# The level products of a gated recurrence, made for 64 of 128 columns

## The chip, the cores and the metric

The kernel runs on one core of a Trainium2 chip. The metric is the device time of one execution in microseconds (us); the runs of the kernel before took 2719.22 to 2722.33 us, with a median of 2722.05 us. In the profile PE is TensorE's matmul, PEld its loading of weights, DVE is VectorE, ACT is ScalarE, POOL is GpSimd and SP is the engine whose queue issues most DMAs.

## The reference

The model has two layers on 1024 tokens of 1024 features, all in fp32. Layer 0 mixes a short convolution with a gated linear recurrence of four heads (128 keys by 128 values each); layer 1 is a retention layer; each is followed by a feed-forward network. Only the recurrence is touched here. For each head and each chunk the reference computes

```python
b = jnp.cumsum(ln, axis=-2)                       # logs of the forget gates, summed along the chunk
diff = b[:, :, :, None, :] - b[:, :, None, :, :]
decay = jnp.exp(jnp.where(causal[:, :, None], diff, -jnp.inf))
scores = jnp.einsum('bhik,bhijk,bhjk->bhij', qn, decay, kn)
o_intra = jnp.einsum('bhij,bhjv->bhiv', scores, vn)
```

so that the score of query i and key j is a sum over 128 keys with a decay of its own for each pair (i, j).

## The kernel before

The tokens are worked on in two halves of 512 (`HT`), and each half in four chunks of 128 (`P`). `mixer0` first projects F (gates), K, Q and V of the half with `four` (lines 331 to 333), then runs the recurrence over the chunks (lines 349 to 423), and after that the convolution's projections (`feat`, lines 426 to 445) and the output products.

The score matrix S of a chunk, with keys j on partitions and queries i along the row, is put together from a diagonal (lines 356 to 359) and from seven levels, `LEVELS` = 1, 2, 4, ..., 64. At the level with spacing s the chunk's 128 tokens are cut into blocks of 2s; in each block the first s tokens act as keys and the last s as queries. The helper `two` gives these two interleaved views of a tile: 64 columns each, in runs of s with a gap of s between them (at s = 64 one run of 64). VectorE and ScalarE write both into one tile, `xs`: x1, the decayed queries, at the columns of the last s (line 369), and x0, the decayed keys, at the columns of the first s (lines 371 and 373).

TensorE then multiplies `xs` by itself, for each head a 128 x 128 product into a quarter of one PSUM bank (lines 375 and 376). `copy_predicated` (line 379) reads from this bank only the 64 columns of the last s, `two(sp)[1]`, and copies into S those that a mask allows. Lines 380 to 384 bring the running products of the gates, SF and F, to the next level, so the chain from level to level runs through VectorE; the products of a level only feed line 379.

In all there are 2 halves x 4 chunks x 7 levels = 56 such groups of 4 matmuls. In the trace each fp32 matmul stands as two records, each with a weight load of its own, so a group is 8 records and the line has 448.

The other products of the kernel (`mm3`, lines 149 to 151) take fp32 values as a sum of two fp32r parts and stand as one record of 512 columns each. Line 199 (in `scales`) multiplies 128 x 128 fp32 weights by a single column of ones, line 181 (in `spread`) multiplies fp32 weights by 512 columns, and line 398 transposes on TensorE.

The order of the instructions on each engine is not written out by hand. A planner takes the program's order as a priority, estimates each instruction's duration, and places on each engine's queue what it expects to be ready. So the convolution's products of lines 149 to 151 stand on TensorE's queue between the groups of line 376, although the code has them after the recurrence. On the chip each queue is then run in that fixed order.

Of the kernel before, what the change touches and what calls it, by code (L numbers as in the profile page):

```python
# [75 lines left out]
def trunk(ctx: ExitStack, tc: tile.TileContext, a: dict, out: bass.AP, decay):  # L76
# [19 lines left out]
    mm, vec, act = nc.tensor.matmul, nc.vector, nc.scalar  # L96
# [56 lines left out]
    def bank(name):  # L153
        return banks[name].tile([P, HT], F32, name=name)

    def rsqrt(x, n):

        it = sm.tile([P, n], I32, name="it")
        vec.tensor_scalar(it, x.bitcast(I32), 1, None, ALU.logical_shift_right)
        yi = sm.tile([P, n], I32, name="yi")  # L160
        vec.tensor_scalar(yi, it, -1.0, float(0x5F3759DF), ALU.mult, ALU.add)
        y = yi.bitcast(F32)
        for _ in range(3):
            t = sm.tile([P, n], F32, name="nt")
            vec.tensor_tensor(t, y, y, ALU.mult)
            u = sm.tile([P, n], F32, name="nu")
            vec.scalar_tensor_tensor(u, t, -0.5, x, ALU.mult, ALU.mult)
            z = sm.tile([P, n], F32, name="nz")
            vec.scalar_tensor_tensor(z, u, 1.5, y, ALU.add, ALU.mult)
            y = z  # L170
        return y
# [124 lines left out]
    def mixer0(ph, odd):  # L296
# [12 lines left out]
        for half in range(NH):  # L309
# [39 lines left out]
            for c in range(NC):  # L349
                first = half == 0 and c == 0  # L350
                cs = slice(c * P, (c + 1) * P)
                Fc, Kc, Qc = F[:, :, cs], K[:, :, cs], Q[:, :, cs]
                SF = ph.tile([P, HEADS, P], F32, name="SF")
                nc.gpsimd.memset(SF, 1.0)
                S = ph.tile([P, HEADS, P], F32, name="S")
                sp = bank("pa").rearrange("p (h i) -> p h i", i=P)
                for m in range(HEADS):
                    mm(sp[:, m], Kc[:, m], Qc[:, m], start=True, stop=True)
                vec.tensor_tensor(S, sp, ident.unsqueeze(1).to_broadcast([P, HEADS, P]), ALU.mult)
                for n, s in enumerate(LEVELS):  # L360
                    nb = P // (2 * s)

                    def two(t):
                        v = t.rearrange("p h (n w s) -> p h n w s", w=2, s=s)
                        return v[:, :, :, 0, :], v[:, :, :, 1, :]

                    xs = ph.tile([P, HEADS, P], F32, name="xs", bufs=3)
                    (x0, x1), (f0, f1), (k0, _), (_, q1), (s0, s1) = map(two, (xs, Fc, Kc, Qc, SF))
                    vec.tensor_tensor(x1, q1, f1, ALU.mult)
                    if s == 1:  # L370
                        act.copy(x0, k0)
                    else:
                        vec.tensor_tensor(x0, k0, s0, ALU.mult)
                    sp = bank("pa").rearrange("p (h i) -> p h i", i=P)
                    for m in range(HEADS):
                        mm(sp[:, m], xs[:, m], xs[:, m], start=True, stop=True)  # L376
                    mk = msk[:, n].rearrange("p (n w s) -> p n w s", w=2, s=s)[:, :, 1, :]
                    last = [P, HEADS, nb, s]
                    vec.copy_predicated(two(S)[1], mk.unsqueeze(1).to_broadcast(last), two(sp)[1])
                    if s == 1:  # L380
                        act.copy(s0, f1)
                    else:
                        vec.tensor_tensor(s0, s0, f1[:, :, :, s - 1 : s].to_broadcast(last), ALU.mult)
                    vec.tensor_tensor(f1, f1, f0[:, :, :, s - 1 : s].to_broadcast(last), ALU.mult)
                qd = ph.tile([P, HEADS, P], F32, name="xs", bufs=3)
                vec.tensor_tensor(qd, Qc, Fc, ALU.mult)
                op = bank("pb")
                for m in range(HEADS):
                    vs = slice(m * P, (m + 1) * P)
                    mm(op[:, vs], S[:, m], V[:, c, vs], start=True, stop=first)  # L390
                    if not first:
                        mm(op[:, vs], qd[:, m], state[:, m], start=False, stop=True)
                if half < NH - 1 or c < NC - 1:
                    kd = ph.tile([P, HEADS, P], F32, name="xs", bufs=3)
                    vec.tensor_tensor(kd, Kc, SF, ALU.mult)
                    tp = bank("pa")
                    for m in range(HEADS):
                        nc.tensor.transpose(tp[:, m * P : (m + 1) * P], kd[:, m], ident)
                    kt = ph.tile([P, HT], F32, name="xs", bufs=3)
                    act.copy(kt, tp)  # L400
                    up = bank("pb")
                    for m in range(HEADS):
                        vs = slice(m * P, (m + 1) * P)
                        mm(up[:, vs], kt[:, vs], V[:, c, vs], start=True, stop=True)
                    if first:
                        vec.tensor_copy(state, up.rearrange("p (h v) -> p h v", v=P))
                    else:
                        for m in range(HEADS):
                            vec.scalar_tensor_tensor(
                                state[:, m], state[:, m], Fc[:, m, P - 1 : P], up[:, m * P : (m + 1) * P], ALU.mult, ALU.add  # L410
                            )
                sq = ph.tile([P, HT], F32, name="t1", bufs=2)
                act.activation(sq, op, AF.Square)
                ss = sm.tile([P, HEADS], F32, name="ss")
                vec.tensor_reduce(ss, sq.rearrange("p (h v) -> p h v", v=P), AX.X, ALU.add)
                ms = sm.tile([P, HEADS], F32, name="ms")
                vec.tensor_scalar(ms, ss, 1.0 / P, EPS, ALU.mult, ALU.add)
                r = rsqrt(ms, HEADS)
                ot = ph.tile([P, HEADS, P], F32, name="on", bufs=4)
                vec.tensor_tensor(  # L420
                    ot, op.rearrange("p (h v) -> p h v", v=P), r.unsqueeze(2).to_broadcast([P, HEADS, P]), ALU.mult
                )
                on.append(ot)
# [694 lines left out]
    def mixer(layer):  # L1118
        with ExitStack() as es:
            if layer == 0:  # L1120
                new_h(0)
                new_h(2)
            es.enter_context(psum(mm=4, pa=2, pb=2))
            new_w(es, 1024, 3)
            new_x(es.enter_context(tc.tile_pool(name=f"mx{layer}", bufs=1, reuse_waits="tile")))
            if layer == 0:
                with tc.tile_pool(name="p0", bufs=1) as ph:
                    start(ph)
            else:
                apply(scaled_h[0], 0, R_MIX + NK)  # L1130
            with tc.tile_pool(name=f"mp{layer}", bufs=1, reuse_waits="tile") as ph:
                with tc.tile_pool(name=f"mo{layer}", bufs=1, reuse_waits="tile") as odd:
                    return (mixer1 if layer else mixer0)(ph, odd)
# [37 lines left out]
```

## Time and profile before

| | before |
|---|---|
| median of 3 runs | 2722.05 us |
| lowest and highest | 2719.22 and 2722.33 us |
| the profiled execution | 2720.06 us |
| its span from first to last instruction | 2718.3 us |
| PE busy | 2640.4 us (97%) |
| DVE busy | 1823.4 us (67%) |
| line 376, PE busy | 60.5 us |

The recurrence of the first half lies at 88 to 168 us of the span and that of the second half at 332 to 409 us. A matmul's busy time in a row overlaps with that of its neighbours, since matmuls are pipelined; the distance between starts, or between ends in the chain, is what one takes from TensorE's time.

### The profile page before, as it was taken

To read this page: it belongs to the slowest core of one execution; us is meant where nothing else is said; L and a number is where in the kernel's file an instruction comes from. 1 tells how busy PE (TensorE), PEld (TensorE's weight loads), DVE (VectorE), ACT (ScalarE), POOL (GpSimd) and SP (SyncE) were. 2 spreads that over 40 slices of the span, in tenths; PEclk is the share of its full clock that TensorE was granted. 3 is DMA by queue.
4 is the path that set the end of the run, shared out by engine and by line. 5 is a ranking of instruction groups with operands and counts; after the bars stand their busy time and mean duration, and the time that the engine had idled before them with its cause. 6 is when DMAs were issued, how large, how long until landed. Compare 5 with 4: busy or idle time off the path is not lost.

```text
span 2718.3 us, 32932 instructions
## 1 busy us (share of the span) xinstructions
PE 2640.4 (97%) x12093; PEld 2180.1 (80%) x12093; DVE 1823.4 (67%) x3387; ACT 1014.0 (37%) x1669; POOL 378.0 (14%) x282
## 2 busy tenths in 40 slices
PE   8999999979999999999999999999998899999998
PEld 6888888757877788878888888888886688888886
DVE  5786497666587666677667667567678666655665
ACT  5223313434434433343332333333344444443332
POOL 0000000042332313200000000000002323231320
PEclk9999999989999999999999999999999999999999
DMA  4224312344434477332322333322224444447742
GB/s 155 78 65 128 95 47 78 116 146 153 160 135 148 163 289 269 130 109 79 92 85 86 94 101 104 104 80 78 85 88 126 167 156 155 146 141 288 269 173 83
DMA packets 320498, 356.28 MB, mean 131 GB/s; under 512 B 11464, under 2 KB 246544, under 8 KB 319312
## 3 DMA queue, kind: packets, MB, share of 16 engines
q1 hardware_dynamic: 317808, 347.13, 38.6%
q0 software_dynamic: 1520, 5.51, 0.6%
q8 instruction: 95, 1.56, 0.2%
q10 hardware_dynamic: 1008, 1.54, 0.2%
q14 instruction: 67, 0.55, 0.1%
HBM read 268.15 MB, written 85.98 MB: 130 GB/s over the span
## 4 chain that ended last, share of the span: by engine, by line
PE 86%; DVE 5%; issue 3%; POOL 2%; DMA 2%; ACT 1%; POOLq 0%; ACTq 0%; DVEq 0%
PE mm L151 15%; PE mm L149 15%; PE mm L150 15%; PE sd L517 6%; PE sd L519 6%; PE sd L518 6%; PE mm L517 5%; PE mm L518 5%; PE mm L519 5%; PE pa L376 2%; POOL s L502 1%; DMA raw<-in_ffn_w_in 1%; DVE wlo L133 1%; DVE st L133 1%; POOL raw L505 1%
## 5 line engine op out<-in xcount | busy, mean ns | idle before, releaser
L136 ACT CAST whi<-raw 128x512 fp32r<-128x512 f32 (+2 forms) x604 | 454.1, 755 | 1115.0 <-PE mm L150 387.6
L133 DVE TENSOR_TENSOR wlo<-raw,whi 128x512 fp32r<-128x512 f32 (+2 forms) x604 | 541.8, 899 | 220.6 <-ACT whi L136 218.6
L149 PE MATMUL mm<-xe,whi 128*128 128x512 f32 x960 | 376.4, 393 | 1.5 <-ACT xe L136 1.5
L150 PE MATMUL mm<-xe,whi 128*128 128x512 f32 x960 | 376.9, 393 | 0.0
L151 PE MATMUL mm<-xe,wlo 128*128 128x512 f32 x960 | 376.3, 392 | 0.0
L517 PE MATMUL sd<-x,whi 128*128 128x512 f32 x640 | 254.0, 397 | 35.5 <-ACT whi L136 21.2
L519 PE MATMUL sd<-x,wlo 128*128 128x512 f32 x640 | 251.3, 393 | 2.4 <-DVE wlo L133 2.4
L518 PE MATMUL sd<-x,whi 128*128 128x512 f32 x640 | 251.7, 393 | 0.4 <-DVE x L133 0.4
L502 POOL TENSOR_TENSOR s<-raw 128x512 f32<-128x512 f32 (+1 forms) x64 | 97.8, 1528 | 986.3 <-DMA raw<-in_ffn_w_in 651.4
L149 PEld LDWEIGHTS mm<-xe,whi 128*128 128x128 f32 x960 | 180.4, 188 | 37.7 <-ACT xe L136 1.7
L151 PEld LDWEIGHTS mm<-xe,wlo 128*128 128x128 f32 x960 | 180.5, 188 | 36.7 <-issue 0.5
L150 PEld LDWEIGHTS mm<-xe,whi 128*128 128x128 f32 x960 | 180.4, 188 | 35.9 <-issue 0.2
L517 PEld LDWEIGHTS sd<-x,whi 128*128 128x128 f32 x640 | 121.5, 190 | 67.5 <-ACT whi L136 23.8
L517 PE MATMUL mm<-xe,whi 128*128 128x512 f32 x440 | 172.6, 392 | 2.8 <-ACT nx L605 2.8
L519 PE MATMUL mm<-xe,wlo 128*128 128x512 f32 x440 | 171.6, 390 | 0.0
L518 PE MATMUL mm<-xe,whi 128*128 128x512 f32 x440 | 171.3, 389 | 0.0
L244 DVE TENSOR_TENSOR h<-h,mm 128x512 f32<-128x512 f32 x128 | 87.8, 686 | 96.5 <-PE mm L151 96.0
L151 PE MATMUL mm<-y,wlo 128*128 128x512 f32 x384 | 149.7, 390 | 0.0
L150 PE MATMUL mm<-y,whi 128*128 128x512 f32 x384 | 149.6, 390 | 0.0
L149 PE MATMUL mm<-y,whi 128*128 128x512 f32 x384 | 149.3, 390 | 0.0
L519 PEld LDWEIGHTS sd<-x,wlo 128*128 128x128 f32 x640 | 121.0, 189 | 28.8 <-DVE wlo L133 3.6
L518 PEld LDWEIGHTS sd<-x,whi 128*128 128x128 f32 x640 | 121.7, 190 | 25.7 <-DVE x L133 0.8
(301 smaller groups left out, 5138.7 us busy)
## 6 DMA issues: line engine op xcount, KB each, us to landing
hid<-st SPq DMA_DIRECT2D x134, 512.0 KB, 3.6
raw<-in_ffn_w_in SPq DMA_DIRECT2D x98, 512.0 KB, 4.8
raw<-in_odd_w_in SPq DMA_DIRECT2D x96, 512.0 KB, 3.8
T<-hid SPq DMA_DIRECT2D x86, 512.0 KB, 6.4
raw<-in_even_w_in SPq DMA_DIRECT2D x56, 512.0 KB, 3.6
xe<-hid SPq DMA_DIRECT2D x48, 512.0 KB, 6.0
raw<-in_odd_w_out SPq DMA_DIRECT2D x32, 512.0 KB, 3.4
raw<-in_ffn_w_out SPq DMA_DIRECT2D x24, 512.0 KB, 5.4
```

What stands on the lines that cost most here:

```text
L133: vec.tensor_tensor(o, x, y, ALU.subtract)
L136: act.copy(hi, src)
L149: mm(o, l[0], r[0], start=first, stop=False)
L150: mm(o, l[0], r[1], start=False, stop=False)
L151: mm(o, l[1], r[0], start=False, stop=last)
L244: vec.tensor_tensor(h(m, ts), h(m, ts), ps, ALU.add)
L376: mm(sp[:, m], xs[:, m], xs[:, m], start=True, stop=True)
L502: pool_add(s1, a21, a22, ALU.add)
L505: pool_add(a11, s1, a11, ALU.add)
L517: mm(ps, wh_, xh, start=start and n == 0, stop=False, skip_group_check=True)
L518: mm(ps, wh_, xl, start=False, stop=False, skip_group_check=True)
L519: mm(ps, wl, xh, start=False, stop=n == len(w) - 1, skip_group_check=True)
```

## The change

In each level the moving operand of the product is now x1, the 64 columns of the queries, instead of all 128 columns of `xs`; the output goes to the 64 columns of the bank that line 379 reads. The stationary operand, which is loaded as weights, stays the whole of `xs`. The other 64 columns of the bank are no longer written, and nothing reads them.

```diff
                     sp = bank("pa").rearrange("p (h i) -> p h i", i=P)
                     for m in range(HEADS):
-                        mm(sp[:, m], xs[:, m], xs[:, m], start=True, stop=True)
+                        mm(two(sp)[1][:, m], xs[:, m], x1[:, m], start=True, stop=True)
                     mk = msk[:, n].rearrange("p (n w s) -> p n w s", w=2, s=s)[:, :, 1, :]
                     last = [P, HEADS, nb, s]
                     vec.copy_predicated(two(S)[1], mk.unsqueeze(1).to_broadcast(last), two(sp)[1])
```

## Rows read from the trace of the kernel before

**Rows 1.** The page: busy time of the engines, us, share of the span, instructions

```profile
PE 2640.4 (97%) x12093; PEld 2180.1 (80%) x12093; DVE 1823.4 (67%) x3387; ACT 1014.0 (37%) x1669; POOL 378.0 (14%) x282
```

**Rows 2.** Busy time by stretch: (window, length, PE, PEld, DVE, ACT, POOL, granted clock, DMA)

```profile
88.00:168.00 80.00, 79.37 (x520) 69.57 (x519) 73.66 (x200) 19.00 (x32) 2.10 (x4) 1.00 0.20 60
168.00:332.00 164.00, 164.00 (x745) 136.06 (x744) 91.37 (x154) 60.72 (x83) 0.00 (x0) 1.00 0.36 106
332.00:409.00 77.00, 77.00 (x507) 67.30 (x505) 70.02 (x196) 14.29 (x22) 1.57 (x3) 1.00 0.17 49
```

**Rows 3.** Groups by line, PE: count, busy us, mean ns of one, idle before

```profile
L376 PE MATMUL pa<-xs 128*128 128x128 f32 x448 | 60.5, 278 | 0.0
L199 PE MATMUL pa<-ones,na 128*128 128x1 f32 x32 | 3.8, 240 | 0.0
```

**Rows 4.** Timeline of weight loads behind a group of line 376 (start, duration, instruction)

```profile
97.51 0.64 PEld L376 LDWEIGHTS pa<-xs 128*128 128x128 f32 x5
98.07 0.19 PEld L150 LDWEIGHTS mm<-xe,whi 128*128 128x128 f32 x1
```

**Rows 5.** The same around line 199

```profile
168.78 0.97 PEld L199 LDWEIGHTS pa<-ones,na 128*128 128x128 f32 x8
169.67 0.19 PEld L149 LDWEIGHTS mm<-xe,whi 128*128 128x128 f32 x1
```

**Rows 6.** Timeline of matmuls around the same group of line 376

```profile
97.29 1.05 PE L376 MATMUL pa<-xs 128*128 128x128 f32 x8
98.10 0.47 PE L150 MATMUL mm<-xe,whi 128*128 128x512 f32 x1
98.41 0.39 PE L151 MATMUL mm<-xe,wlo 128*128 128x512 f32 x1
```

**Rows 7.** The same around line 199

```profile
168.88 0.95 PE L199 MATMUL pa<-ones,na 128*128 128x1 f32 x8
169.70 0.48 PE L149 MATMUL mm<-xe,whi 128*128 128x512 f32 x1
170.02 0.39 PE L150 MATMUL mm<-xe,whi 128*128 128x512 f32 x1
```

**Rows 8.** Chain of work around the group of line 376 (from end to end)

```profile
97.21 0.23 PE mm L149
97.45 0.89 PE pa L376 x8
98.34 0.23 PE mm L150
```

**Rows 9.** Chain of work around line 199

```profile
169.05 0.79 PE pa L199 x8
169.84 0.34 PE mm L149
170.18 0.23 PE mm L150
```

**Rows 10.** Chain of work: two fp32 records of 512 columns

```profile
186.97 0.86 PE pb L181 x2
```

**Rows 11.** Line 376: who waited for it (us, times)

```profile
  DVE S L379: 1.2, 5
  PEld pa L376: 1.1, 5
```

**Rows 12.** Timeline: two groups of line 376, with the operand write before each

```profile
109.03 0.42 DVE L369 TENSOR_TENSOR xs<-big 128x256 f32<-128x256 f32 x1
109.76 1.05 PE L376 MATMUL pa<-xs 128*128 128x128 f32 x8
111.44 0.41 DVE L369 TENSOR_TENSOR xs<-big 128x256 f32<-128x256 f32 x1
111.58 0.39 PE L149 MATMUL mm<-xe,whi 128*128 128x512 f32 x1
112.00 1.13 PE L376 MATMUL pa<-xs 128*128 128x128 f32 x8
```

**Rows 13.** Waits of PE, whole span (us, times, longest us): the two longest

```profile
PE sd L517 <- ACT whi L136: 21.2, 6, 7.3
PE sd L517 <- ACT sd L705: 12.6, 6, 2.5
```

## The prediction

> **What bounds the kernel now.** I read the busy times first: PE has work for 97% of the span, and no other engine comes near [rows 1]. Then the stretches: in the two recurrences PE is busy for 79.4 of 80 us and for all of 77 us, while DVE has 73.7 and 70.0 us of work in them; between the recurrences PE is busy for 164 of 164 us [rows 2]. So the chain from level to level on VectorE is covered: the convolution's products fill TensorE's queue between the groups of line 376. In these stretches time is gained by less work on TensorE, and lost by any standstill of it, because no gap behind them could take the work in. [...]
>
> Line 376 is the line to be changed; its 448 records have 60.5 us of busy time [rows 3]. Busy times overlap, so what a record takes has to be read from the distance between starts. There the reader should look at two things side by side: a group of line 376, with 128 moving columns, and line 199, which has the same 128 x 128 fp32 weights and one moving column.
>
> **What a record costs.** In the group, five weight loads start at 97.51 us and the next line's load at 98.07 us: 0.56 / 5 = 0.112 us each [rows 4]. For line 199, eight loads start at 168.78 us and the next at 169.67 us: 0.89 / 8 = 0.111 us each [rows 5]. One column or 128, a record takes 0.11 us. Is that the weights or the columns? Two fp32 records of 512 columns take 0.86 us [rows 10], so a column costs 0.86 / 1024 = 0.00084 us; 128 columns are 0.107 us, 64 are 0.054 us, one is 0.001 us. At 128 columns the streaming (0.107) and the weight load (0.111) are nearly equal; under 128 columns the weight load decides, and the change leaves it as it is.
>
> **The change part by part.**
>
> *Removed: 64 of 128 columns of 448 records.* By streaming alone that would be 448 x 0.054 = 24 us. By the weight loads it is nothing. To be sure that time doesn't come back at the group's edge, take the whole stretch from the first record's start to the second 512-column product behind the group: 98.41 - 97.29 = 1.12 us with 128 columns [rows 6], 170.02 - 168.88 = 1.14 us with one column [rows 7]. No row has 64 columns; it lies between these two, and I take zero. The bounds for the 56 groups are 0.02 x 56 = 1.1 us to either side, which is the reading's own error.
>
> *Moved: the end of a group.* In the chain the eight records with 128 columns end at 98.34 us and the next product 0.23 us later [rows 8]; the eight with one column end at 169.84 us and the next product 0.34 us later [rows 9]. So the last record's result is there 0.11 us sooner with one column, and the queue behind it gains nothing from that. For 64 columns I take half, 0.05 us. Line 379 is the only reader. It was seen waiting for line 376 five times, 1.2 us in all [rows 11]; 5 x 0.05 = 0.3 us is what VectorE gains, and 1.2 us would be the most. Does that reach TensorE? Only where TensorE itself stands for the next operand. That happens: at 112.00 us a group starts 0.42 us after the product before it instead of 0.23 us, right behind the operand's write, which ended at 111.85 us [rows 12]. I give the change these 0.3 us; the bounds are 0 and 1.2 us.
>
> *Added: runs and gaps.* The moving operand and the output now go through two views in runs of s, with gaps. No matmul of this kernel does so now, so no row has its price. From below it is nothing: at 0.054 us for 64 columns the streaming has 0.111 / 0.054 = 2.07 times its own length before it shows behind the weight load. From above I let a column cost four times as much: 64 x 0.00084 x 4 = 0.215 us a record, 0.103 us over the weight load. At s = 1 alone, where no two columns are neighbours, this is 64 records x 0.103 = 6.6 us; at s = 1, 2 and 4 it is 19.8 us; at all six levels with gaps 39.6 us. I take nothing, since fp32 columns stream at half the rate of the fp32r products (512 columns every 0.23 us [rows 8], against 0.43 us here [rows 10]), which leaves slack both in the rate and under the load.
>
> [...]
>
> *Waits.* None is added or taken away: the weight load of the first head still needs the whole of `xs`, and nothing reads the columns left unwritten.
>
> *The order.* The planner estimates a product of 64 columns as shorter, or at least as ending sooner, so it may place a 512-column product more or fewer ahead of a group, and from there on other things may shift. TensorE's work stays the same; only standstills can change. This costs nothing as long as a group finds its operand written: the group at 109.76 us starts 0.31 us after its operand's write ended at 109.45 us, while the one that stood started 0.15 us after it [rows 12]. The spare time is thus about 0.16 us, less than one 512-column product (0.23 us).
>
> **Sum.** The profiled execution took 2720.06 us, of which 2718.3 us are the span. Minus 0.3 us makes 2719.8 us. The median of the runs lies 2722.05 - 2720.06 = 1.99 us above the profiled execution, so the forecast is 2721.8 us: no change that can be measured. A measurement of this kernel tells 0.2% from no change, which is 5.4 us, or 2716.6 to 2727.5 us.
>
> **Rivals.**
>
> *Columns count after all (faster).* If the pace of 0.11 us at one column came from something particular to line 199, and line 376 were paced by its columns, each record would fall to the 0.054 us of its streaming: 448 x (0.111 - 0.054) = 25.5 us less, 2696 us. For it: 128 columns stream in 0.107 us, close to the 0.111 us seen. Against it: line 199's loads keep the same pace with hardly any streaming [rows 4, 5]. I give 0.07.
>
> *The order comes out worse (slower).* One 512-column product fewer stands ahead of each group, and TensorE stands for the operand. Its place is the head of each of the 56 groups, its price 0.23 - 0.16 = 0.07 us for a group with the spare time above and 0.23 us for one without: 3.9 to 12.9 us. It decides from the point where the planner takes more than those 0.16 us out of a group's cover. What stands is lost, since TensorE has no gap for it up to 332 us [rows 2]. That gives 2726 to 2735 us; 2731 in the middle. For it: the queue's order is fixed and the spare time is short. Against it: VectorE's chain, which sets when operands come, is nearly untouched. I give 0.09.
>
> *The order comes out better (faster).* Standstills later in the span shrink when the order shifts. TensorE waits 21.2 and 12.6 us in its two largest waits, in the feed-forward stages [rows 13]; a third of these would be 11 us, 2711 us. For it: these waits are there to be gained. Against it: the change touches nothing near them. I give 0.07.
>
> *Gaps cost (slower).* [...] I give 0.06.
>
> That the change doesn't do what it says would look like the forecast itself and needs no case of its own.
>
> **How the numbers follow.** The forecast has 0.71. Its own range is 1.1 us of reading, 1.2 us of gain and some 3 us of small shifts in the order: 2717 to 2726 us. Faster by over 0.2%: columns 0.07 and better order 0.07, 0.14. Slower by over 0.2%: worse order 0.09 and gaps 0.06, 0.15. Within: 0.71. For the range I reach down to 2711 us, the better order, and up to 2731 us, the middle of the worse order and gaps at s = 1. Left out are the columns (0.07) and the upper parts of the two slower rivals (about 0.08).
>
> **What the profile after would show.** The records of line 376 with 64 columns, their weight loads still 0.11 us apart, and the stretch from a group's first start to the second product behind it still about 1.12 us: the forecast's main step. A stretch of 0.7 us or less would mean that columns count. Loads over 0.11 us apart at s = 1 and not at s = 64 would mean that gaps cost. Group ends that move up by 0.05 us, with waits of line 379 a little shorter, confirm the small gain. PE's busy share of the two recurrences should stay at 99 to 100%; if the pace is kept and PE stands at the groups' heads, the order was it. The forecast is wrong if the time moves by over 5.4 us either way.

## The result and the profile after

| | before | after |
|---|---|---|
| median | 2720.99 us (6 runs) | 2744.06 us (6 runs) |
| lowest and highest | 2719.22 and 2722.33 us | 2741.64 and 2745.83 us |
| the profiled execution | 2720.06 us | 2741.64 us |
| its span | 2718.3 us | 2739.9 us |

The changed kernel is slower: the ratio is 1.0081 with a 95% interval of 1.0069 to 1.0093, 23 us. The forecast was 2721.8 us, no change, with a range up to 2731 us: the measured time lies 13 us above that range. The line of the product is now 377, and the lines behind it have moved down by one.

**Where the time went.** The first product of line 585, which opens the feed-forward stage, starts at 531.3 us instead of 509.6 us (line 584 before). That is 21.7 us of the 21.6 us by which the span grew, so all of it was lost ahead of that point, in layer 0's mixer. The next two fences have the busy time of that stage: first before, then after (window, its length, PE, PEld, DVE, ACT, POOL, granted clock, DMA).

```profile
88.00:510.00 422.00, 420.75 (x2221) 355.56 (x2220) 297.39 (x662) 130.58 (x189) 3.67 (x7) 1.00 0.28 84
```

```profile
88.00:532.00 444.00, 431.05 (x2222) 365.46 (x2222) 299.24 (x662) 130.77 (x189) 3.67 (x7) 0.97 0.27 80
```

The work is the same (2221 and 2222 records), and DVE's busy time hardly moved. PE stood still for 422.00 - 420.75 = 1.25 us before and for 444.00 - 431.05 = 12.95 us after, 11.7 us more. Its busy time grew by 431.05 - 420.75 = 10.3 us for the same work, and the granted clock fell from 1.00 to 0.97: the trace has 0.50 instead of 1.00 for part of the stage. 11.7 + 10.3 = 22.0 us. The 0.50 was granted in four stretches, 3.4, 3.4, 10.2 and 6.8 us, 24 us in all, each beginning in a standstill of TensorE or within 1.0 us behind its end (standstills of 1.61 and 0.37 us at the first, 2.04, 2.14 and 2.23 us at the others); the longest is

```profile
424.60:434.80 10.20, 8.12 (x37) 7.99 (x38) 4.39 (x11) 0.00 (x0) 0.00 (x0) 0.50 0.19 53
```

By recurrence, from the first start of the level products to the last, the first one grew from 77.2 to 88.6 us and the second from 75.4 to 88.6 us. Not all of that is lost: 15.2 us of these 24.6 us are products that moved in from behind the recurrences (counted below). After (compare [rows 2]):

```profile
88.00:177.00 89.00, 85.48 (x534) 74.85 (x533) 74.61 (x200) 21.56 (x35) 1.57 (x3) 0.98 0.20 60
341.00:431.00 90.00, 85.86 (x535) 75.79 (x533) 73.07 (x198) 16.69 (x25) 1.57 (x3) 0.96 0.18 54
```

**The product itself did what was forecast.** A timeline of TensorE in the changed kernel shows a group at s = 64, without a gap, and one at s = 1, with a gap behind every column:

```profile
99.14 1.00 PE L377 MATMUL pa<-xs 128*128 128x64 f32 x8
99.95 0.48 PE L151 MATMUL mm<-xe,wlo 128*128 128x512 f32 x1
100.26 0.39 PE L149 MATMUL mm<-xe,whi 128*128 128x512 f32 x1
...
105.58 1.00 PE L377 MATMUL pa<-xs 128*128 128x64 f32 x8
106.39 0.48 PE L149 MATMUL mm<-xe,whi 128*128 128x512 f32 x1
106.70 0.39 PE L150 MATMUL mm<-xe,whi 128*128 128x512 f32 x1
```

From the first start to the second product behind it both take 1.12 us, which is what 128 columns took [rows 6]. The eight records end 0.05 us sooner than before (1.00 us instead of 1.05 us). So in these groups 64 columns cost TensorE as much as 128, gaps cost nothing, and a group's result comes 0.05 us earlier.

**What is new is who waits.** The waits of line 377 in the changed kernel (the first lines: what ended the idle time ahead of it; behind them: who waited for it):

```profile
  issue: 8.0, 8
  DVE xs L369: 5.3, 4
  PE mm L151: 2.1, 3
  DVE xs L373: 1.6, 2
  DVE nu L167: 0.2, 1
...
  DVE S L380: 17.9, 31
  PEld pa L377: 5.4, 3
```

Before, line 379 had waited for the products 1.2 us in five places [rows 11]; now, as line 380, it waits 17.9 us in 31. TensorE in turn waits 5.3 and 1.6 us for the operand's writes, which stand behind such waits on VectorE's queue. The end of the second recurrence shows both and their consequence (TensorE's timeline):

```profile
420.25 1.00 PE L377 MATMUL pa<-xs 128*128 128x64 f32 x8
421.06 0.48 PE L150 MATMUL mm<-xe,whi 128*128 128x512 f32 x1
421.38 0.40 PE L151 MATMUL mm<-xe,wlo 128*128 128x512 f32 x1
422.19 1.08 PE L377 MATMUL pa<-xs 128*128 128x64 f32 x8 [0.42 <-DVE xs L369]
425.41 1.94 PE L377 MATMUL pa<-xs 128*128 128x64 f32 x8 [2.14 <-DVE xs L369]
428.62 1.94 PE L377 MATMUL pa<-xs 128*128 128x64 f32 x8 [1.28 <-DVE xs L373]
```

and VectorE's in the same place:

```profile
427.38 0.44 DVE L380 COPY_PREDICATED S<-msk,pa 128x256 f32<-128x256 uint8 x1 [1.33 <-PE pa L377]
427.72 0.42 DVE L369 TENSOR_TENSOR xs<-big 128x256 f32<-128x256 f32 x1
428.06 0.42 DVE L373 TENSOR_TENSOR xs<-big,SF 128x256 f32<-128x256 f32 x1
```

Nothing stands between the last groups on TensorE's queue. Each group waits for its operand, VectorE's copy stands ahead of the next operand's writes and waits for the group, and so the two engines take turns. After the standstill at 423 us the same eight records take 1.94 us instead of 1.00 us; the granted clock from 421 to 431 us is 0.68.

**The queues' order.** Nobody changed it by hand; the planner did. Counted on TensorE's queue in the built programs, between the first and the last group of a recurrence, the products of lines 149 to 151 are

| kernel | first recurrence | second recurrence | copies ahead of the next level's x1 |
|---|---|---|---|
| before | 160 | 158 | 31 of 48 |
| after | 192 | 192 | 41 of 48 |

The planner lets 32 and 34 more products of 0.23 us into the recurrences, 7.4 and 7.8 us of work, as if the groups had become shorter. On the chip they have not.

192 is eight times 24, the products of one output (eight blocks of features, three products each), and no run put more than 192 into a recurrence. Behind the last of them in the second recurrence TensorE has none for 18 us, from 421.8 us on, and the next one then waits for VectorE:

```profile
439.61 0.80 PE L149 MATMUL mm<-xe,whi 128*128 128x512 f32 x1 [0.57 <-DVE t L445]
```

Counted in the trace of the changed kernel, TensorE stands at the heads of 7 of the 56 groups, 7.0 us in all, and 5.0 us of that lie at three groups that have no such product between themselves and the group before. In the trace of before it stands at none for more than 0.05 us, and from each recurrence's second chunk on every group has at least two such products ahead of it.

### The profile page after: what moved, and what is told of

It reads as the page before. It is cut to its first block, busy times and chain, and to the rows that moved or that the text cites. A ratio compares the mean times of both kernels' runs of the same rounds, so it can differ in the third digit from the quotient of the medians.

```text
span 2739.9 us, 32934 instructions
## 1 busy us (share of the span) xinstructions
PE 2651.8 (97%) x12093; PEld 2190.7 (80%) x12093; DVE 1825.0 (67%) x3387; ACT 1014.7 (37%) x1669; POOL 377.1 (14%) x282
## 4 chain that ended last, share of the span: by engine, by line
PE 72%; DVE 4%; issue 3%; POOL 2%; DMA 2%; ACT 1%; ACTq 0%; POOLq 0%; DVEq 0%
PE mm L150 11%; PE mm L151 11%; PE mm L149 11%; PE sd L518 6%; PE sd L520 6%; PE sd L519 6%; PE mm L518 5%; PE mm L519 5%; PE mm L520 5%; DMA raw<-in_ffn_w_in 1%; POOL s L503 1%; DVE wlo L133 1%; POOL raw L506 1%; PE pa L988 1%; DVE st L133 1%
```

## The experiments

Two theories stood at the start. **Order**: the 22 us come from the order in which the queues now stand. **Product**: the new product costs it, through its gaps or through the clock. Within the first, two candidates were kept apart: the **fillers** (the products let into the recurrences on TensorE's queue) and the **copy at the head** (the predicated copy ahead of the next operand on VectorE's queue). To pin an order means that on each engine every instruction is tied behind the one that preceded it in the other kernel's built program, by edges of the planner that add no wait.

**p1: 64 columns in the old order.** The changed kernel, all five engines pinned in the order of the kernel before (`_pin` ties each instruction behind its predecessor in a recorded list).

```diff
         trunk(tc, aps, out, decay)
+        _pin(nc, tc)
```

> The changed kernel, with each engine's instructions pinned one behind the other in the order that they have in the kernel before; nothing else differs. Theory 'order' (the 22 us come from the order in which the queues stand, since the planner takes the 64-column products to end sooner): 2716 to 2724 us, like before, granted clock 1.00 in both recurrences. Rival 'product' (64 columns in runs with gaps, or the clock falling when fewer columns stream, cost the time themselves): 2738 to 2747 us, like the changed kernel.

Measured: 2720.61 us, ratio 0.9999 (0.999 to 1.0008). Busy time of its recurrences:

```profile
86.00:164.00 78.00, 77.50 (x509) 68.13 (x507) 72.57 (x199) 19.23 (x32) 1.58 (x3) 1.00 0.21 62
330.00:407.00 77.00, 77.00 (x508) 67.59 (x507) 70.28 (x196) 14.22 (x22) 1.57 (x3) 1.00 0.17 49
```

PE is busy for 77.50 of 78 and for all of 77 us, at a granted clock of 1.00. The recurrences last 76.8 and 75.1 us against 77.2 and 75.4 us: 0.7 us together is what 64 columns bring, and it can't be told from the noise of the whole. The new product costs nothing.

**p2: 128 columns in the new order**, the mirror: the kernel before, pinned in the order of the changed one by the same call.

> The mirror: the kernel before, with its 128-column products, each engine's instructions pinned in the order of the changed kernel. [...] Rival 'product': 2718 to 2724 us.

Measured: 2740.63 us, ratio 1.0071 (1.0055 to 1.0088), within the 2738 to 2750 us of "order" and outside the 2718 to 2724 us of "product". Its recurrences:

```profile
88.00:177.00 89.00, 85.40 (x531) 74.50 (x529) 74.52 (x200) 21.17 (x34) 1.58 (x3) 0.98 0.20 59
341.00:431.00 90.00, 85.96 (x533) 75.52 (x532) 72.89 (x197) 16.59 (x25) 1.58 (x3) 0.97 0.18 54
```

These are the changed kernel's lines almost to the digit, clock included, without a single 64-column product. With p1 this settles it: the order makes the loss, and "product" falls.

**p3: 64 columns, the copy late.** One pair of edges per level: the last level's copy (`held`) stands behind this level's writes of x0 (`w0`) and x1 (`w1`).

```diff
+                        queue_after(held, w0)
+                        queue_after(held, w1)
...
-                    vec.copy_predicated(two(S)[1], mk.unsqueeze(1).to_broadcast(last), two(sp)[1])
+                    held = vec.copy_predicated(two(S)[1], mk.unsqueeze(1).to_broadcast(last), two(sp)[1])
```

> The changed kernel, with one edge per level: on VectorE's queue the predicated copy of a level stands behind the two writes of the next level's operand; the planner orders the rest. Theory 'copy at the head' (the part of the order that matters is the predicated copy standing ahead of the next level's operands, so that VectorE waits for TensorE at every level): DVE's waits for line 376's products fall from 17.9 us to under 4 us and the time to 2715 to 2726 us. Rival 'fillers' (what matters is which 512-column products stand between the groups, and when their weights are split): the time stays over 2732 us although the waits shrink.

Measured: 2735.96 us, ratio 1.0059 (1.0044 to 1.0074). VectorE's wait for the products fell to 11.1 us in 14 places, not under 4, and 8 of the 23 us came back. The built program still had 188 and 192 fillers. The time stayed over 2732 us although the waits shrank, which is what "fillers" expected; "copy at the head" alone doesn't hold.

**p4: 128 columns, the copy first.** The reverse edge in the kernel before: the update of the gates' products (`u`) stands behind this level's copy.

```diff
+                    queue_after(u, held)
```

> The kernel before, 128 columns, with one edge per level: the predicated copy of a level stands ahead of that level's update of the gates' products (and with it ahead of the next level's operands); the planner orders the rest. Theory 'copy at the head': VectorE waits for TensorE at most of the 56 levels, some 15 to 25 us in all, and the time is 2735 to 2750 us. Rival 'fillers': the planner knows of the edge and places other work into the wait, so the time stays at 2716 to 2728 us.

Measured: 2750.98 us, ratio 1.0114 (1.0099 to 1.013): VectorE waited 19.7 us in 27 places for the products, and PE 7.9 us in 6 for the operand. Here too the planner had put 192 and 192 fillers into the recurrences. So a copy ahead of the next operands, together with the plan that came with it, costs 30 us with the whole 128 columns, though the planner knew of the edge and was free to fill the wait. The run doesn't part the copy from the fillers.

**p5 and p6: one queue pinned.** 64 columns, with only TensorE's queue (p5) or only VectorE's (p6) in the old order.

> The changed kernel with only TensorE's queue pinned in its old order (160 and 158 products of 512 columns between the first and the last group of line 376 in the two recurrences); the planner orders the other queues, and the predicated copy stands ahead of the next level's x1 in 39 of 48 cases, as in the changed kernel (41). Theory 'fillers' (the time lies in the 192 and 192 products that the planner lets into the recurrences): 2716 to 2727 us. Theory 'copy at the head' (VectorE's queue): over 2734 us.

> The changed kernel with only VectorE's queue pinned in its old order; the planner orders TensorE's queue and again lets 192 and 192 products of 512 columns into the recurrences. Theory 'fillers': 2733 to 2747 us. Theory 'copy at the head': 2716 to 2727 us.

Measured: 2738.77 us for p5 (1.0067, 1.0051 to 1.0082) and 2735.61 us for p6 (1.0057, 1.0042 to 1.0072). Under each of the two candidates one of these runs should have cured the loss, and neither did. In p5, with the old 160 and 158 fillers, line 377 is short of its operand all along (idle time of its engine, and by whom it ended; then who waited):

```profile
  issue: 16.5, 18
  DVE xs L369: 8.3, 8
  DVE xs L373: 2.2, 5
  PE mm L151: 2.1, 3
...
  DVE S L380: 10.7, 28
```

In p6 the copies are back in their old places, and they still wait:

```profile
  DVE S L380: 14.5, 31
```

now with 192 fillers on TensorE's queue. In p5 TensorE stands at 15 heads of groups, 10.7 us in all; in p6 at 4, 2.3 us. The two queues have to fit each other: an old queue beside a new one cost 16 to 19 us here.

**p7: half a dose.** Two heads of four with 64 columns.

```diff
-                        mm(two(sp)[1][:, m], xs[:, m], x1[:, m], start=True, stop=True)
+                        if m < 2:
+                            mm(two(sp)[1][:, m], xs[:, m], x1[:, m], start=True, stop=True)
+                        else:
+                            mm(sp[:, m], xs[:, m], xs[:, m], start=True, stop=True)
```

> A half dose: two of the four heads with 64 columns, the other two with 128; the planner lets 185 and 172 products of 512 columns into the recurrences. Theory 'fillers': between the two kernels, by the surplus of (25 + 14) of (32 + 34) products about 0.6 of the 22 us, 2729 to 2741 us. If any disturbance of the order costs the same, however small: about 2740 us; if the time hangs on something that only the full change brings: 2718 to 2725 us.

Measured: 2723.65 us, ratio 1.0011 (1.0001 to 1.002), inside the range for "something that only the full change brings". It is a miss for "fillers" as a sum: 0.6 of the surplus made 3.5 of the 23 us. Nor does every disturbance cost the same. The loss is not proportional to the count. Busy time of its recurrences:

```profile
87.20:169.80 82.60, 81.88 (x526) 72.29 (x525) 73.75 (x198) 20.53 (x34) 1.58 (x3) 1.00 0.21 64
336.70:414.50 77.80, 77.31 (x505) 69.08 (x504) 70.56 (x194) 15.23 (x23) 1.57 (x3) 1.00 0.17 48
```

PE hardly stands in them (81.88 of 82.60 and 77.31 of 77.80 us busy) and the granted clock stays at 1.00, though VectorE waits 7.5 us in 25 places for the products. From each second chunk on every group has at least two fillers ahead of it, and TensorE stands at one head, for 0.5 us; its longest standstill, 3.0 us, comes behind the first recurrence.

**p8: 64 columns in the second half alone** (`if half == 1`, otherwise as p7).

> 64 columns in the second half's recurrence alone, 128 in the first; the planner lets 160 and 192 products of 512 columns into the two. Theory 'fillers': the first recurrence lasts 76 to 78 us as before, the second 86 to 90 us as in the changed kernel, and the time is 2731 to 2738 us (the second half's share of the 22 us was 13 us). If the loss is a chance shift of the whole order: no relation to the half.

Measured: 2731.84 us, ratio 1.0042 (1.0027 to 1.0057). The first recurrence lasted 76.8 us, the second 88.6 us, the very lengths of the old and of the new order. Stretch up to the second recurrence, and the second with what follows:

```profile
88.00:332.00 244.00, 243.73 (x1270) 206.29 (x1269) 165.17 (x354) 80.70 (x117) 2.10 (x4) 1.00 0.30 90
332.00:432.00 100.00, 93.04 (x570) 82.18 (x569) 76.75 (x209) 18.46 (x29) 1.57 (x3) 0.94 0.18 52
```

The loss stays in the half that has the narrow products.

**p9: other columns left out.** The run from column s on, which holds all queries: 127 columns at s = 1, 64 at s = 64.

```diff
-                        mm(sp[:, m], xs[:, m], xs[:, m], start=True, stop=True)
+                        mm(sp[:, m, s:], xs[:, m], xs[:, m, s:], start=True, stop=True)
```

> Another way to leave columns out: the moving operand is the run of columns from s on (127 at s = 1 down to 64 at s = 64), without gaps, whole weights, the planner's own order. All that line 379 reads is written. The planner lets 160 and 165 products of 512 columns into the recurrences (160 and 158 before). Theory 'planner counts columns, chip pays weights': a group still takes its 1.12 us from its first start to the second product behind it at every s, and since the order hardly moves the time stays at 2715 to 2728 us. Rival 'any edit of this product loses': over 2730 us.

Measured: 2721.77 us, ratio 1.0005 (0.9996 to 1.0014). No gain, no loss; the plan kept its shape (160 and 165), and at s = 64 a group still takes 1.12 us from its first start to the second product behind it. Leaving out columns (14% of them here, half in the change) isn't harmful by itself; what counts is how far the plan moves.

**p10: columns and weights left out.** p9, and the weights end where the keys end.

```diff
-                        mm(sp[:, m, s:], xs[:, m], xs[:, m, s:], start=True, stop=True)
+                        mm(sp[: P - s, m, s:], xs[:, m, : P - s], xs[:, m, s:], start=True, stop=True)
```

(The mask, S and the copy of line 379 are cut to the same rows.)

> As p9, and the weights are cut too: the stationary operand is the run of columns up to 128 - s (64 of 128 at s = 64, 96 at s = 32, 127 at s = 1), which holds all keys; the predicated copy takes only those rows. The planner's own order, the same counts as p9. Theory 'a record takes what its weight load takes': groups at s = 64 take about half of their 0.89 us, at s = 32 three quarters; summed over the seven levels 0.98 of a group per chunk, 8 x 0.98 x 0.89 = 7.0 us less than p9, so 2708 to 2722 us. Rival 'a fixed 0.11 us per record, whatever is loaded': like p9.

Measured: 2716.73 us, ratio 0.9982 (0.9973 to 0.9991), faster than both kernels and 5.0 us under p9. TensorE's timeline at s = 64:

```profile
122.93 0.68 PE L376 MATMUL pa<-xs 128*64 128x64 f32 x8
123.54 0.50 PE L151 MATMUL mm<-xe,wlo 128*128 128x512 f32 x1
123.88 0.40 PE L149 MATMUL mm<-xe,whi 128*128 128x512 f32 x1
```

From the first start to the second product behind it are 0.95 us instead of 1.12 us: half of the weights, and the group gives back 0.17 us. Columns alone gave nothing (p9), columns with weights do: the weights set the pace. Of the expected 7 us 5 came by the medians; in the traces the groups' stretches are 4.2 us shorter in sum than in p9, mainly because at s = 64 a group gave back 0.17 us and not half of its 0.89 us.

**p11 and p12: 64 columns with the cut weights**, in the old order (p11) and in the planner's own (p12).

```diff
-                        mm(two(sp)[1][:, m], xs[:, m], x1[:, m], start=True, stop=True)
+                        mm(two(sp)[1][: P - s, m], xs[:, m, : P - s], x1[:, m], start=True, stop=True)
```

(The mask and the copy are cut as in p10.)

> 64 moving columns as in the changed kernel, weights cut as in p10, every engine pinned in the order of the kernel before. Theory 'a record takes what its weight load takes': s = 64 groups at about half; 2710 to 2718 us, and the recurrences 2 to 4 us shorter where PE is the later engine, else filled by standstills of PE. Rival 'fixed 0.11 us': 2717 to 2724 us, as the same order with whole weights.

> p11 with the planner's own order: 64 moving columns and cut weights; it lets 192 and 192 products of 512 columns into the recurrences, the counts of the changed kernel, so the cut of the weights does not show in the plan. Theory 'the order makes the loss': 2730 to 2744 us, some of the 7 us of weights gained, the loss still there.

Measured: 2717.86 us for p11 (0.9992, 0.9983 to 1.0001), inside what both theories allow, so its time decides nothing; its groups at s = 64 take 0.92 to 0.95 us from the first start to the second product behind, as in p10. 2740.03 us for p12 (1.0066, 1.005 to 1.0083): in the planner's order the loss is there again. p12's counts are those of the changed kernel, 192 and 192, and so is the number of fillers between any two groups, which says that the plan moved with the moving columns and not with the weights.

## Why the prediction was wrong

**The cost of a record** was right, and for the reason given: the weight load paces it, 1.12 us for a group with 64 columns as with 128. So were the group's end (0.05 us sooner), the size of the gain (0.3 us forecast; 0.7 us in p1, where the order is held) and the price of gaps (none). The rivals "columns count after all" and "gaps cost" fell with the same lines. No run shows the prediction's column that costs four times as much in runs with gaps, on which its 6.6 us at s = 1, a part of the range's upper end, and the 0.06 of "gaps cost" stand: the group at s = 1, where no two written columns are neighbours, takes 1.12 us like the one at s = 64, and p1, with the gaps in the old order, took 2720.61 us. What gaps do to a product paced by its columns, no run here tells.

**The step that failed is "The order".** It saw that the planner might take the product for shorter, and then priced that at one 512-column product ahead of a group, 0.07 to 0.23 us each, 12.9 us at most, with a chance of 0.09. Three things were wrong in it.

- *How far the plan moves.* The step let it move by one product here or there. It moved by 32 and 34 products over the two recurrences. The prediction itself had the number that bounds this: 24 us of streaming were "removed" that the chip does not give back. A plan that counts columns thinks it has them, 12 us in each recurrence, and by estimate 12 / 0.23 is room for 52 products. It took the 192 that there were, and the groups behind them stood bare.
- *Which queue.* The reason against the rival was that VectorE's chain "is nearly untouched". It wasn't: the copies moved ahead of the next level's operands, from 31 to 41 of 48, and line 380 waits 17.9 us. Setting back this queue alone (p6) or TensorE's alone (p5) did not take the loss away.
- *The clock.* A standstill was priced at its own length. Here 11.7 us of it came with 10.3 us more of busy time for the same work, in a stage with 24 us at a granted clock of 0.50. This was no part of any rival's sum.

The rival's sign was right; its price, 3.9 to 12.9 us, was mis-sized against 23 us. Its place was right in part: it had a short standstill at the head of each of the 56 groups, where TensorE stood 7.0 us at 7 heads, up to 2.1 us at one; the other 4.7 us lie elsewhere, mostly behind the recurrences. And it was no rival to the forecast but its consequence: the same fact that makes the change worth nothing on the chip, that weights and not columns are paid (1.12 us a group at s = 64 with 128 or 64 columns, 0.95 us with half of the weights), makes the plan wrong if it counts columns.

**What stays open.** That the plan moved because the planner counts columns is an inference from the built orders (counts that rise with narrower products, no change with narrower weights), not from its estimates, which weren't read. And within the pair of queues no single placement was shown to make the loss; p7 says that it isn't the count alone. What the traces share is the bare heads: from the second chunk of a recurrence on, groups with no filler ahead of them are found in the changed kernel, p2, p3, p4, p6, p8 (second half) and p12, all of which lost, and none in the kernel before, p1, p7 and p9 to p11, which lost at most 3.5 us. p5 lost without them, with TensorE's old queue beside a new one on VectorE. No run moved fillers to those heads alone, so this is argued and not shown.

## What to carry to other kernels

Where a planner orders the queues by estimated durations, an edit is two edits: what it does to the engine and what it does to the estimate; an edit that is worth nothing on the chip can still cost time, here 23 us. Pin the old order on the new kernel and the new order on the old one: two runs tell the two apart. And to shorten a stream of small fp32 products, cut what paces them, here the weights (p10: 0.95 us instead of 1.12 us for a group at s = 64).

## What the runs showed of the hardware that was not expected

In p10 fewer weight columns quickened a group, but the products behind it gave part of that back. TensorE's weight loads in p10 at s = 64 (64 weight columns, 64 moving columns):

```profile
122.93 0.54 PEld L376 LDWEIGHTS pa<-xs 128*64 128x64 f32 x8 [0.36 <-issue]
123.54 0.19 PEld L151 LDWEIGHTS mm<-xe,wlo 128*128 128x128 f32 x1
```

Record by record these loads start 0.058 us apart, against 0.111 us with 128 weight columns, but the next line's load starts 0.2 us behind the last of them. The first and the last of the eight records of the product start 0.46 us apart, and 0.95 us lie between the group's first start and the second product behind it. With 128 weight columns and 128 moving ones it is 0.78 us (7 x 0.111) of 1.12 us [rows 4, 6]. So 0.32 us less in the group were 0.17 us less on the engine. Why the next load comes late, no run here shows.
